# SSD sample block: stored-state and new-state products moved from the whole array to 32-wide strips

## The chip, the cores and the metric

The kernel runs on one core of a Trainium2 chip. The metric is the device time of one launch in microseconds (us). The kernel before took 1897.55 us, the median of three runs that went from 1896.7 to 1902.05 us.

## The reference

One step of a one-layer trunk is computed for 1024 new prompt rows and for 8 running streams of 16 rows each (128 sample rows, one block of 128). Three mixers run on the same normalised input: a stick-breaking attention, a Mamba-2 SSD group and a forgetting attention (FoX). Then come an output projection, a cross-attention into memory tokens, a SwiGLU feed-forward part and a last norm. Everything is float32.

The change touches the SSD mixer, and of it only the sample block. For a stream b and a head h with 64 channels p, a state of 128 numbers n, and the 16 rows t of the stream, the reference computes

```python
h0 = past['ssm']                                             # (8 streams, 8 heads, 64, 128)
y_off = einsum('bcthn,bchpn->bcthp', C, h_in) * exp(a_cum)   # what the stored state gives
chunk_states = einsum('bcshn,bcsh,bcshp->bchpn', B, to_end, x)
h_final = chunk_decay * h0 + chunk_states                    # the new state, an output
```

B and C are shared by the four heads of a group; there are two groups. So each stream has two products with its stored state (one for each group: 16 rows of C by 4 heads x 64 channels, contracted over the 128 state numbers) and, for the new state, a contraction over its 16 rows.

## The kernel before

The kernel is written with a tile framework: the program gives instructions in an order, and a planner, which runs a timeline of its own with costs for every instruction, sets the final order on each engine's queue. Instructions written earlier have the higher priority. `together` (L332) raises a list of matmuls far ahead in priority and has all but the first issued on the engine behind the first, so that they come out side by side. Buffers come from pools with a fixed number of slots; a tile takes a slot that is free and gives it back after its last reader. The PSUM pools matter here: `pd` has two banks (PD = 2), `pT` has three (PT_ = 3), `pS` two and `pO` one (L40). All DMAs are issued from one queue, SP's.

The attention of the prompt and of the streams (`pipeline`, L631) gives one step after another; between these steps L1296 to L1300 draw steps from a filler: first the remaining dense projections, then `ssd_gen` (L968). `ssd_gen` takes the sample block (i = 8) first and then the prompt blocks 0 to 7. For each block: `load` brings the conv output, the cumulated decays (as a broadcast from the scratch `ac_sc`, L1040) and the gate; `prepare` transposes; `weights` builds the decay weights (L1071 to L1087); `states` is the part with the stored state; `outputs` and `write` end it. The SBUF pool of `act` tiles has six slots; the two `st8` tiles with the stored states of four streams each are two of them, and a later block's load can take their slots only when the new states have been stored from them (L1145).

In `states`, for the sample block (L1104 to L1148), `cps[g]` is a zeroed 128 x 1024 area in which the 16 columns of C of stream b stand in a window of 128 columns for that stream, at the stream's own place among the 128 rows of the block. For each half hf of four streams:

- `bms` (L1121, POOL): B with the rows of all other streams zeroed, four streams side by side, 128 x 512, for each of the two groups. The area is used again in the second half.
- for each stream four transposes into a `pT` bank (L1129), an ACT copy to SBUF (L1131), and two products (L1133) that accumulate in the `pd` bank `yo` over all eight streams: a stationary 128 x 128 (mostly zeros) against 256 moving columns, each writing all 128 rows.
- for each of four head pairs j one product (L1140), 128 rows contracted, 128 x 128 stationary, 512 moving columns (four streams), into a `pd` bank, and four DVE instructions (L1143) that scale the old state and add the new part in place.
- one store of the half's 1 MB of new states (L1145).

A plain float32 matmul leaves two records in the trace, each with its weight load; a transpose leaves one. In the attention, `prompt_av` (L595) already issues products on two column strips of 64 and the stream attention (L874, L934) and the cross-attention (L1562) on four column strips of 32, all through `together`.

Of the kernel before, what the change touches and what calls it, by code (L numbers as in the profile page):

```python
# [12 lines left out]
ALU = mybir.AluOpType  # L13
# [4 lines left out]
P = 128  # L18
# [4 lines left out]
DEC_S = 16  # L23
# [39 lines left out]
def tile_hybrid_step(ctx: ExitStack, tc: tile.TileContext, a: dict):  # L63
    nc = tc.nc
    ACT, DVE, POOL, PE, SP = nc.scalar, nc.vector, nc.gpsimd, nc.tensor, nc.sync
# [20 lines left out]
    def act_t(dt=F32R, home=None):  # L86
        return (home or actp).tile([P, 3072], dt, tag="act", name="act")
# [13 lines left out]
    def sg_t(dt=F32):  # L101
        return sgp.tile([P, 512], dt, tag="sg", name="sg")
# [4 lines left out]
    def ps_t(pool, tag):  # L107
        return pool.tile([P, 512], F32, tag=tag, name="ps" + tag)

    def pd():  # L110
        return ps_t(psd, "d")
# [4 lines left out]
    def pT():  # L116
        return ps_t(pst, "t")
# [11 lines left out]
    def pool_tt(out, in0, in1, op):  # L129

        for a0, a1 in pieces_of(out.shape[1]):
            POOL.tensor_tensor(out=out[:, a0:a1], in0=in0[:, a0:a1], in1=in1[:, a0:a1], op=op)  # L132
# [19 lines left out]
    ident = cst.tile([P, P], F32, name="ident")  # L152
# [44 lines left out]
    maskh = mcst.tile([P, 2], F32, name="maskh")  # L197
# [134 lines left out]
    def together(emits):  # L332

        with tc.high_priority(GROUP):
            first = emits[0]()
            with tc.issue_after(first.ins):
                for f in emits[1:]:
                    f()
# [629 lines left out]
    def ssd_gen():  # L968
# [3 lines left out]
        bmask = sc[:, 1536:1544]  # L972
# [17 lines left out]
        for t_, pat in ((bo3, [0, DEC_S]), (bmask, None)):  # L990
            for sgn, base in ((-1, 0), (1, DEC_S - 1)):
# [6 lines left out]
                          in1=negA.unsqueeze(1).to_broadcast([P, NBLK, 8]), op=ALU.mult)  # L998
        POOL.tensor_copy(avx.rearrange("p (h d) -> p h d", d=64),
                         av[:, 64:72].unsqueeze(2).to_broadcast([P, 8, 64]))  # L1000
        ps = pd()
# [12 lines left out]
        ps = pd()  # L1014
# [7 lines left out]
        def h3(t):  # L1022
            return t.rearrange("p (h d) -> p h d", h=8)

        def bc(col, n=64):
            return col.unsqueeze(2).to_broadcast([P, 8, n])

        def heads_tt(out, x, col):

            for a0, a1 in pieces_of(512):  # L1030
                POOL.tensor_tensor(out=out[:, a0:a1].rearrange("p (h d) -> p h d", d=64),
                                   in0=x[:, a0:a1].rearrange("p (h d) -> p h d", d=64),
                                   in1=col[:, a0 // 64:a1 // 64].unsqueeze(2).to_broadcast([P, (a1 - a0) // 64, 64]),
                                   op=ALU.mult)

        def load(i):
            A = act_t(F32)
            SP.dma_start(out=A[:, 0:1024].rearrange("p (j t) -> p j t", t=P),
                         in_=xbc_sc[:, i * P:(i + 1) * P].rearrange("(j p) t -> p j t", p=P))
            SP.dma_start(out=A[:, 1024:2048],  # L1040
                         in_=ac_sc[8 * i:8 * i + 8, :].rearrange("h t -> (h t)").unsqueeze(0).to_broadcast([P, 1024]))
            SP.dma_start(out=A[:, 2048:2560], in_=z_sc[i * P:(i + 1) * P, :])
            return A

        def views(A, B):
            xT = A[:, 0:1024].rearrange("p (j t) -> p j t", t=P)
            return (xT, A[:, 1024:2048], A[:, 2048:2560], B[:, 0:256], B[:, 256:512],
                    *(B[:, 512 + 512 * k:1024 + 512 * k] for k in range(4)))
# [40 lines left out]
        def states(i, A, B, t1):  # L1089
            xT, br, zt, Bn, cb, xn, xd, xe, xD = views(A, B)  # L1090
            hs = slice(8 * i, 8 * i + 8)
            if i < 8:
                ps = pd()
                for g in range(2):
                    PE.matmul(ps[:, g * 256:(g + 1) * 256], xT[:, 6 + g, :], hT[:, g * 256:(g + 1) * 256],
                              start=True, stop=True)
                DVE.tensor_tensor(out=h3(t1), in0=h3(ps), in1=bc(ea[:, hs]), op=ALU.mult)
                heads_tt(hT, hT, dec[:, hs])
                ps = pd()
                for g in range(2):  # L1100
                    PE.matmul(ps[:, g * 256:(g + 1) * 256], Bn[:, g * P:(g + 1) * P], xe[:, g * 256:(g + 1) * 256],
                              start=True, stop=True)
                DVE.tensor_tensor(out=hT, in0=hT, in1=ps, op=ALU.add)
            else:  # L1104
                hs_, cps = [], []
                for g, t in enumerate(st8):
                    hst = t[:, :2048].rearrange("p (u n) -> p u n", n=P)

                    cp = t[:, 2048:3072]
                    POOL.memset(cp, 0.0)  # L1110
                    cv = bass.AP(cp.tensor, cp.offset, [list(cp.ap[0]), [144, 8], [1, 16]])
                    POOL.tensor_copy(cv, xT[:, 6 + g, :].rearrange("p (b t) -> p b t", t=DEC_S))
                    hs_.append(hst.rearrange("p (b j) n -> p b j n", j=4))
                    cps.append(cp)
                yo = pd()
                for hf in range(2):
                    hst = hs_[hf]
                    bms = []
                    for g in range(2):
                        bm = (A, B)[g][:, 2560:3072]  # L1120
                        POOL.tensor_tensor(out=bm.rearrange("p (b n) -> p b n", n=P),  # L1121
                                           in0=Bn[:, g * P:(g + 1) * P].unsqueeze(1).to_broadcast([P, 4, P]),
                                           in1=bmask[:, 4 * hf:4 * hf + 4].unsqueeze(2).to_broadcast([P, 4, P]), op=ALU.mult)
                        bms.append(bm)
                    for b in range(4):
                        bb = 4 * hf + b
                        tp = pT()
                        for j in range(4):
                            PE.transpose(tp[:, j * P:(j + 1) * P], hst[:, b, j, :], ident)  # L1129
                        h0 = sg_t()  # L1130
                        ACT.copy(h0, tp)  # L1131
                        for g in range(2):
                            PE.matmul(yo[:, g * 256:(g + 1) * 256], cps[g][:, bb * P:(bb + 1) * P],  # L1133
                                      h0[:, g * 256:(g + 1) * 256], start=bb == 0 and g == 0, stop=bb == 7,
                                      skip_group_check=True)
                        if b % 2 == 1:
                            yield
                    for j in range(4):
                        ps = pd()
                        PE.matmul(ps, xe[:, j * P:(j + 1) * P], bms[j // 2], start=True, stop=True)  # L1140
                        for b in range(4):
                            bb = 4 * hf + b
                            DVE.scalar_tensor_tensor(hst[:, b, j, :], hst[:, b, j, :], dcol[:, 8 * j + bb:8 * j + bb + 1],  # L1143
                                                     ps[:, b * P:(b + 1) * P], ALU.mult, ALU.add)
                    SP.dma_start(out=a["s_ssm"][0, 4 * hf:4 * hf + 4].rearrange("b h p n -> (b h p) n")  # L1145
                                 .rearrange("(u p) n -> p u n", p=P), in_=hst.rearrange("p b j n -> p (b j) n"))
                    yield
                DVE.tensor_tensor(out=h3(t1), in0=h3(yo), in1=bc(ea[:, hs]), op=ALU.mult)  # L1148
            pool_tt(t1, t1, xD, ALU.add)
# [23 lines left out]
        A, nxt = load(order[0]), None  # L1173
        B = act_t(F32)
# [8 lines left out]
        for n, i in enumerate(order):  # L1183
# [3 lines left out]
            if i == 7:  # L1187
                ps = pd()
# [18 lines left out]
            if n < 8:  # L1207
# [3 lines left out]
                A, B = A1, B1  # L1211
# [517 lines left out]
    B = {}  # L1729
# [335 lines left out]
```

## Time and profile before

| | |
|---|---|
| runs without a profile | 1897.55 us (1896.7 to 1902.05) |
| the profiled execution | 1900.41 us, of which the span of the profile is 1897.6 us |
| TensorE busy, as the profile counts it | 1832.7 us of the span |
| DVE, ACT, POOL busy | 890.6, 822.0, 618.0 us |
| stored-state products L1133 | 32 records, from 543.9 to 563.8 us |
| new-state products L1140 | 16 records, from 548.7 to 570.9 us |

PE is TensorE, PEld its weight loads, DVE VectorE, ACT ScalarE, POOL GpSimd and SPq the queue from which the DMAs are issued. A busy PE is not a PE at its peak, because the ends of pipelined matmuls are modelled: what a group of matmuls costs is read from the start of its first record to the start of the next instruction, not from its own duration. Windows are given in us from the start of the span.

### The profile page before, as it was taken

How to read it: one execution, taken by the hardware profiler on the slowest of the kernel's cores; microseconds unless marked ns; L12 is line 12 of the kernel's file. 1: busy time of each engine (PE TensorE's matmuls, PEld its weight loads, DVE VectorE, ACT ScalarE, POOL GpSimd, SP SyncE). 2: the span in 40 equal slices, each digit the busy share in tenths (PEclk: the TensorE clock that was granted, in tenths of full speed). 3: DMA queues.
4: the chain of work that ended last, by engine and by line, in shares of the span. 5: the costliest groups of instructions: out<-in, count | busy, mean ns of one | idle time of the engine just before them, and what ended most of it. 6: DMA issues, size and time to landing. Idle time of an engine off the chain costs nothing.

```text
span 1897.6 us, 32376 instructions
## 1 busy us (share of the span) xinstructions
PE 1832.7 (97%) x12120; PEld 1637.1 (86%) x12120; DVE 890.6 (47%) x1802; ACT 822.0 (43%) x1751; POOL 618.0 (33%) x923
## 2 busy tenths in 40 slices
PE   7999989999988899999999989999999999999998
PEld 5899878888966767899988879999999999788886
DVE  3412332566556863444444586333333333355554
ACT  6533543545567662344332474333333333344443
POOL 7622434535116652111112107445444542000000
PEclk9999999999999999999999999999999999999999
DMA  9464753537768773345576124333222233656572
GB/s 339 143 189 148 219 153 111 167 94 211 223 199 277 242 254 114 111 134 173 173 278 210 64 76 110 81 87 77 70 70 70 70 79 100 210 181 236 180 241 89
DMA packets 291069, 296.64 MB, mean 156 GB/s; under 512 B 80092, under 2 KB 242884, under 8 KB 290912
## 3 DMA queue, kind: packets, MB, share of 16 engines
q1 hardware_dynamic: 290912, 294.57, 49.6%
q8 instruction: 95, 1.56, 0.3%
q14 instruction: 62, 0.51, 0.1%
HBM read 225.12 MB, written 69.91 MB: 155 GB/s over the span
## 4 chain that ended last, share of the span: by engine, by line
PE 81%; DMA 7%; DVE 4%; POOL 4%; issue 2%; ACT 2%; SPq 1%; POOLq 0%; DVEq 0%; ACTq 0%
PE psd L1867 11%; PE psd L328 9%; PE psd L329 9%; PE psd L330 9%; PE pst L1867 8%; PE pss L1867 4%; PE pss L328 3%; PE pss L329 3%; PE pss L330 3%; POOL wl L132 2%; PE pso L1867 2%; PE pst L328 2%; PE pst L329 1%; PE pso L595 1%; PE pst L330 1%
## 5 line engine op out<-in xcount | busy, mean ns | idle before, releaser
L132 POOL TENSOR_TENSOR wl<-wr,wh 128x256 fp32r<-128x256 f32 (+2 forms) x184 | 138.8, 788 | 232.7 <-ACT wh L292 228.1
L330 PE MATMUL psd<-act,wl 128*128 128x384 f32 x528 | 180.8, 343 | 0.7 <-POOL wl L132 0.7
L328 PE MATMUL psd<-act,wh 128*128 128x384 f32 x528 | 181.4, 344 | 0.0
L329 PE MATMUL psd<-act,wh 128*128 128x384 f32 x528 | 180.7, 342 | 0.0
L1867 PE MATMUL pst<-bT,tr 128*128 128x256 f32 (+1 forms) x1068 | 155.0, 293 | 0.0
L1867 PEld LDWEIGHTS pst<-bT,tr 128*128 128x128 f32 x1068 | 144.9, 188 | 0.1
L330 PE MATMUL psd<-wh,act 128*128 128x512 f32 (+3 forms) x424 | 136.1, 322 | 0.0
L329 PE MATMUL psd<-wl,act 128*128 128x256 f32 (+3 forms) x414 | 133.5, 323 | 1.1 <-POOL wl L132 1.1
L328 PE MATMUL psd<-wh,act 128*128 128x256 f32 (+3 forms) x414 | 132.7, 324 | 1.2 <-DMA act<-osc 1.1
L1867 PE MATMUL psd<-bT,tr 128*128 128x320 f32 (+1 forms) x912 | 132.8, 295 | 0.6 <-POOL tr L132 0.6
L1867 PEld LDWEIGHTS psd<-bT,tr 128*128 128x128 f32 x912 | 124.8, 188 | 1.0 <-POOL tr L132 0.9
L132 POOL TENSOR_TENSOR tr<-u,tr 128x256 fp32r<-128x256 f32 x110 | 82.5, 779 | 101.2 <-ACT tr L1703 83.3
L253 POOL TENSOR_SCALAR sm<-sm 128x1 f32<-128x1 f32 (+2 forms) x27 | 7.1, 261 | 299.9 <-ACT y L1969 211.7
L1842 DVE TENSOR_TENSOR tr<-tr,pst 128x256 f32<-128x256 f32 (+1 forms) x86 | 38.6, 449 | 139.7 <-ACT tr L1839 106.4
L330 PEld LDWEIGHTS psd<-act,wl 128*128 128x128 f32 x528 | 99.2, 188 | 3.4 <-issue 1.9
L132 POOL TENSOR_TENSOR ws<-ws 128x256 f32<-128x256 f32 (+2 forms) x100 | 69.8, 725 | 98.3 <-DVE ws L522 85.2
L328 PEld LDWEIGHTS psd<-act,wh 128*128 128x128 f32 x528 | 99.4, 188 | 2.1 <-issue 1.6
L329 PEld LDWEIGHTS psd<-act,wh 128*128 128x128 f32 x528 | 99.3, 188 | 1.9 <-issue 1.5
L132 POOL TENSOR_TENSOR tr<-raw,tr 128x256 fp32r<-128x256 f32 x94 | 69.2, 766 | 83.6 <-ACT tr L1703 75.3
L1703 ACT CAST tr<-tr 128x384 fp32r<-128x384 f32 (+1 forms) x70 | 37.7, 538 | 117.3 <-DMA tr<-hidsc 114.0
L292 ACT CAST wh<-wr 128x512 fp32r<-128x512 f32 (+2 forms) x90 | 52.3, 621 | 81.3 <-PE psd L330 31.9
L328 PEld LDWEIGHTS psd<-wh,act 128*128 128x128 f32 x414 | 78.8, 191 | 9.9 <-issue 2.0
(637 smaller groups left out, 4763.5 us busy)
## 6 DMA issues: line engine op xcount, KB each, us to landing
u<-w_down SPq DMA_DIRECT2D x40, 512.0 KB
raw<-w_down SPq DMA_DIRECT2D x26, 512.0 KB
st<-qksc SPq DMA_DIRECT2D x48, 256.0 KB
wr<-w_in SPq DMA_DIRECT2D x44, 256.0 KB
tr<-hidsc SPq DMA_DIRECT2D x57, 192.0 KB
hidsc<-tr SPq DMA_DIRECT2D x34, 288.0 KB
qksc<-sg SPq DMA_DIRECT2D x48, 192.0 KB
wr<-cache_sb_k SPq DMA_DIRECT2D x32, 256.0 KB
```

The source lines that it names most:

```text
L132: POOL.tensor_tensor(out=out[:, a0:a1], in0=in0[:, a0:a1], in1=in1[:, a0:a1], op=op)
L253: POOL.tensor_scalar(v, ss, inv, EPS, ALU.mult, ALU.add)
L292: ACT.copy(hi, raw)
L328: PE.matmul(out, ah, bh, start=start, stop=False)
L329: PE.matmul(out, ah, bl, start=False, stop=False)
L330: PE.matmul(out, al, bh, start=False, stop=stop)
L595: return PE.matmul(po[r:r + 64, q_], vt[:, 2 * (k0 + i) + j, :], pfs[i][:, sl], start=start and k0 == 0 and (j == 0 or qp > 0), stop=k0 + ...
L1703: ACT.copy(hi, src)
L1842: DVE.tensor_tensor(out=at(out, g), in0=at(x, g), in1=ps[g][:, :GW[g]], op=op)
L1867: PE.matmul(dst[g][:, :GW[g]], x[:, ka], y[:, k, :], start=start and k == 0 and m == 0, stop=stop and k == 3 and m == 2, skip_group_check= ...
```

## The change

The new `states` for the sample block, of which only this part differs:

```diff
-                    cp = t[:, 2048:3072]
+                    cp = t[:, 2048:2304]
                     POOL.memset(cp, 0.0)
-                    cv = bass.AP(cp.tensor, cp.offset, [list(cp.ap[0]), [144, 8], [1, 16]])
-                    POOL.tensor_copy(cv, xT[:, 6 + g, :].rearrange("p (b t) -> p b t", t=DEC_S))
+                    cv = bass.AP(cp.tensor, cp.offset, [list(cp.ap[0]), [64, 4], [48, 2], [1, 16]])
+                    POOL.tensor_copy(cv, xT[:, 6 + g, :].rearrange("p (i e t) -> p i e t", e=2, t=DEC_S))
...
+                bms = []
+                for g in range(2):
+                    bm = (A, B)[g][:, 2560:2816]
+                    POOL.tensor_tensor(out=bm.rearrange("p (e n) -> p e n", n=P),
+                                       in0=Bn[:, g * P:(g + 1) * P].unsqueeze(1).to_broadcast([P, 2, P]),
+                                       in1=maskh.unsqueeze(2).to_broadcast([P, 2, P]), op=ALU.mult)
+                    bms.append(bm)
                 for hf in range(2):
                     hst = hs_[hf]
-                    bms = []
-                    for g in range(2):
-                        bm = (A, B)[g][:, 2560:3072]
-                        POOL.tensor_tensor(out=bm.rearrange("p (b n) -> p b n", n=P),
-                                           in0=Bn[:, g * P:(g + 1) * P].unsqueeze(1).to_broadcast([P, 4, P]),
-                                           in1=bmask[:, 4 * hf:4 * hf + 4].unsqueeze(2).to_broadcast([P, 4, P]), op=ALU.mult)
-                        bms.append(bm)
-                    for b in range(4):
-                        bb = 4 * hf + b
-                        tp = pT()
-                        for j in range(4):
-                            PE.transpose(tp[:, j * P:(j + 1) * P], hst[:, b, j, :], ident)
-                        h0 = sg_t()
-                        ACT.copy(h0, tp)
-                        for g in range(2):
-                            PE.matmul(yo[:, g * 256:(g + 1) * 256], cps[g][:, bb * P:(bb + 1) * P],
-                                      h0[:, g * 256:(g + 1) * 256], start=bb == 0 and g == 0, stop=bb == 7,
-                                      skip_group_check=True)
-                        if b % 2 == 1:
-                            yield
+                    for e in range(2):
+                        h0 = []
+                        for b in (e, 2 + e):
+                            tp = pT()
+                            for j in range(4):
+                                PE.transpose(tp[:, j * P:(j + 1) * P], hst[:, b, j, :], ident)
+                            h0.append(sg_t())
+                            ACT.copy(h0[-1], tp)
+                        together([lambda r=32 * (2 * hf + x), g=g, x=x: PE.matmul(
+                            yo[r:r + 32, g * 256:(g + 1) * 256], cps[g][:, 2 * r + 32 * e:2 * r + 32 * e + 32],
+                            h0[x][:, g * 256:(g + 1) * 256], start=e == 0 and g == 0, stop=e == 1, skip_group_check=True)
+                            for g in range(2) for x in (1, 0)])
+                        yield
                     for j in range(4):
-                        ps = pd()
-                        PE.matmul(ps, xe[:, j * P:(j + 1) * P], bms[j // 2], start=True, stop=True)
+                        pss_ = [pd(), pT()]
+                        together([lambda r=32 * (2 * hf + x), x=x: PE.matmul(
+                            pss_[x][:, :256], xe[r:r + 32, j * P:(j + 1) * P], bms[j // 2][r:r + 32, :],
+                            start=True, stop=True) for x in range(2)])
```

Two neighbouring streams share a strip of 32 rows. For the products with the stored state, C of a stream stands in a window of 32 columns (the other stream's 16 are zero), and the result goes to the 32 rows of the strip alone. The two streams that are taken together lie in different strips: streams 0 and 2, then 1 and 3, and likewise in the second half. For the new state, only the 32 rows of the strip are contracted, against B with one of the two streams zeroed in each half of 256 columns (`maskh` in place of `bmask`); the two strips of a half write to two banks, one from `pd` and one from `pT`. The DVE instructions keep their number and shape and read from the two banks in turn. B is masked once for all streams and both halves. The number of transposes, copies, steps of the filler and DMAs stays as it was; there are eight more `pT` tiles, sixteen new-state matmuls in place of eight, and the products are issued through `together`.

More of the change, by code (lines that the diff above doesn't have):

```diff
@@ L1143, in states @@
                             DVE.scalar_tensor_tensor(hst[:, b, j, :], hst[:, b, j, :], dcol[:, 8 * j + bb:8 * j + bb + 1],
-                                                     ps[:, b * P:(b + 1) * P], ALU.mult, ALU.add)
+                                                     pss_[b // 2][:, b % 2 * P:(b % 2 + 1) * P], ALU.mult, ALU.add)
                     SP.dma_start(out=a["s_ssm"][0, 4 * hf:4 * hf + 4].rearrange("b h p n -> (b h p) n")
```

## The prediction

> **What bounds the kernel now.** I read the page first, then the busy time by stretches of ten microseconds around the sample block, then the order of PE's instructions there, then what PE and the DMA queue wait for.
>
> ```profile
> PE 1832.7 (97%) x12120; PEld 1637.1 (86%) x12120; DVE 890.6 (47%) x1802; ACT 822.0 (43%) x1751; POOL 618.0 (33%) x923
> ...
> PE 81%; DMA 7%; DVE 4%; POOL 4%; issue 2%; ACT 2%; SPq 1%; POOLq 0%; DVEq 0%; ACTq 0%
> ```
>
> Over the whole span PE sets the time: work taken from PE is worth its length wherever nothing else ends later. The chain is 19% other things, though, and the sample block lies in a stage where these matter:
>
> ```profile
> core 0: us, PE busy (x) PEld busy (x) DVE busy (x) ACT busy (x) POOL busy (x), PEclk, DMA share, GB/s
> 500.00:740.00 240.00, 219.06 (x1659) 171.38 (x1658) 146.16 (x405) 145.47 (x313) 111.49 (x183) 0.96 0.74 235
> ...
> 530.00:540.00 10.00, 6.19 (x47) 4.94 (x45) 5.83 (x25) 7.45 (x21) 5.46 (x8) 0.94 0.64 194
> 540.00:550.00 10.00, 9.71 (x41) 7.28 (x42) 5.60 (x20) 5.02 (x11) 0.00 (x0) 0.72 0.24 61
> 550.00:560.00 10.00, 9.24 (x112) 7.11 (x111) 7.25 (x25) 4.03 (x9) 1.04 (x1) 1.00 0.59 169
> 560.00:570.00 10.00, 10.00 (x52) 6.30 (x51) 6.79 (x24) 9.79 (x21) 2.46 (x3) 1.00 1.04 274
> 570.00:580.00 10.00, 8.10 (x63) 6.72 (x62) 3.69 (x12) 5.01 (x10) 4.05 (x7) 1.00 0.97 314
> ```
>
> From 500 to 740 us PE is idle for 240 - 219 = 21 us, a third of all its idle time (1897.6 - 1832.7 = 65). Before 540 it stands still, then has a low clock; from 560 on the DMA engines are full (1.04, 0.97). PE's order there, with the idle time ahead of an instruction in brackets:
>
> ```profile
> 540.29 0.58 PE L562 MATMUL pss<-st 128*128 128x256 f32 x1 [4.09 <-DVE sm L536]
> ...
> 543.94 2.73 PE L1133 MATMUL psd<-sg,act 128*128 128x256 f32 x8
> 546.32 0.58 PE L562 MATMUL pss<-st 128*128 128x512 f32 x1
> ...
> 552.79 1.12 PE L1140 MATMUL psd<-act 128*128 128x512 f32 x2
> ...
> 556.77 1.10 PE L1140 MATMUL psd<-act 128*128 128x512 f32 x2 [0.76 <-DVE so L959]
> ...
> 572.76 1.31 PE L889 MATMUL pst<-ident,wr 128*128 128x128 f32 x8 [1.32 <-DMA wr<-cache_fox_k]
> ```
>
> So the block's products lie between three stops of PE: 4.09 us before 540.29, 0.76 before 556.77 and 1.32 before 572.76.
>
> **The change part by part.** First what the products cost now. The time of a group runs from its start to that of the next instruction:
>
> ```profile
> 558.14 1.03 PE L1133 MATMUL psd<-sg,act 128*128 128x256 f32 x4
> 559.00 0.60 PE L1129 MATMUL pst<-ident,act 128*128 128x128 f32 x4
> 559.44 0.49 PE L580 MATMUL pst<-ident,ws 128*128 128x128 f32 x3
> ...
> 560.63 1.02 PE L1140 MATMUL psd<-act 128*128 128x512 f32 x2
> 561.49 0.59 PE L1133 MATMUL psd<-sg,act 128*128 128x256 f32 x2
> ```
>
> Four records of L1133 take 559.00 - 558.14 = 0.86 us, 0.215 each; two of L1140 take 561.49 - 560.63 = 0.86, 0.43 each. Thus 32 records of the first cost 6.9 us and 16 of the second 6.9. The first eight of L1133 ran at the low clock: 546.32 - 543.94 = 2.38 instead of 1.72.
>
> *Stored-state products.* After the change they are still 32 records of 256 moving columns, in four groups of eight, each on two column strips in turn. Two column strips in turn are in the trace, in the prompt's attention:
>
> ```profile
> 525.89 1.08 PE L595 MATMUL pso<-pt,st 128*64 128x256 f32 x8
> 526.90 0.88 PE L580 MATMUL pst<-ident,ws 128*128 128x128 f32 x6
> 527.71 0.65 PE L595 MATMUL pso<-pt,st 128*64 128x256 f32 x4
> 528.28 0.65 PE L580 MATMUL pst<-ident,ws 128*128 128x128 f32 x4
> ...
> 895.56 1.07 PE L1562 MATMUL pss<-kf,ws 128*32 128x256 f32 x16
> 896.56 0.39 PE L328 MATMUL pss<-kt,st 128*128 128x256 f32 x1
> ```
>
> Eight records take 526.90 - 525.89 = 1.01, four take 0.57. Half of the serial time would be 0.86 and 0.43; so each group pays 0.14 to 0.15 on top. Strips of 32 do it too: L1562 has sixteen records on four strips in 1.00. Price: 4 x 1.01 = 4.0; saved 3 x (1.72 - 1.01) = 2.1, and for the group at the low clock 2.38 x (1 - 1.01/1.72) = 1.0, together **3.1 us**. Bounds: a loss of 0.6 (four times 0.15) if nothing overlaps, a gain of 3.4 + 0.3 (half of 6.9, and half of the low clock's 0.66) if all does.
>
> The Trainium skill, TensorEngine Tiling (Array Packing), section Key Properties, has a rule against this: changing the tiling mode drains the array. The 0.14 us on each group of L595 is what this trace shows beside it, and it is in the price already, twelve times for the twelve new groups; without it the saving would be 1.7 us larger.
>
> *New-state products.* After the change there are 32 records (16 matmuls) of 256 moving columns in eight groups of four, on two row strips of 32 with 128 stationary columns. No row has two row strips side by side. The nearest by shape is a single matmul with 32 rows, in a stretch with clock 0.50:
>
> ```profile
> 283.11 0.79 PE L726 MATMUL psd<-so,hsel 32*128 32x128 f32 x2
> 283.83 0.80 PE L562 MATMUL pss<-st 128*128 128x512 f32 x1
> ```
>
> Its two records take 0.72 us at half speed, 0.36 at full, where two of 0.11 (L1129's transposes: 0.44 for four) and a group's 0.14 make the same: a row strip is no slower in itself. Ends: no overlap, 32 x 0.215 + 8 x 0.14 = 8.0, a loss of 1.1; full overlap 3.4, a gain of 3.4. I take the column strips' four-record group, 0.57, as nearest in shape of group: 8 x 0.57 = 4.6, saved **2.3 us**.
>
> *What lies beside other work.* POOL's masks and memsets:
>
> ```profile
> L1121 POOL TENSOR_TENSOR act<-act x4: 1038/1039/1039, 537.0 to 561.8; 128x512 f32<-128x512 f32 x4
> ...
>   PE psd L1140: 15.0, 1
> ...
> L1110 POOL MEMSET act<- x2: 950/1196/1442, 511.2 to 520.6; 128x1024 f32 x2
> ```
>
> Four masks of 1.04 become two of half the size, and the memsets shrink to a quarter: about 2 x 1.2 x 3/4 + 4.2 - 1.1 = 4.9 us less on an engine that is busy 2.46 of 10 us here. The 15.0 us that the second half's mask waited for the last product on the old one disappears; but its last mask ended at 562.8, and the second half's first product started at 565.37 (quoted below), so nobody waited for it: zero. Without that cover one mask, 1.04, would be at stake. DVE's 32 instructions (L1143, 0.28 us from start to start), the transposes, copies and DMAs stay: zero.
>
> *What of the 5.4 us is kept.* Up to the stop at 556.77 the cut is two stored-state groups (1.0 + 0.7) and two new-state groups (0.6): 2.3 us. There the DMA share is 0.24 and 0.59, and what the stop waits for (L959 on DVE) comes from PE's own stream attention, which moves up with the rest: I keep all. Behind it the cut is 1.4 + 6 x 0.29 = 3.1 us, and it runs into a stop on a load:
>
> ```profile
> 565.37 1.02 PE L1140 MATMUL psd<-act 128*128 128x512 f32 x2
> ...
> 565.56 7.06 DMA wr<-cache_fox_k
> ...
> 574.28 7.19 DMA s_ssm<-act
> 581.53 0.38 SPq L1038
> 581.96 6.43 DMA act<-acsc
> ```
>
> With full DMA engines the 7.06 us of that load do not start earlier just because PE asks earlier; PE would wait longer than 1.32. What can move is the second store of the states: the chain runs over it and the load into its slot to 588.4. I keep a quarter, 0.8. Sum: 2.3 + 0.8 = **3.1 us**. The profiled execution took 1900.41 us (2.8 outside its span), so 1897.3 in its like; the median of the runs is 2.9 lower than that execution, so **1894.5**.
>
> **The rivals.** *(a) The stop at 540 goes with it.* The planner lays this stage out anew. PE's 4.09 us wait for FoX's DVE work (L536), which stands on DVE behind L1080, which waits for `ac_sc`:
>
> ```profile
> L1080 DVE TENSOR_SCALAR act<-act x45: 268/279/1002, 538.1 to 667.6; 128x128 f32<-128x128 f32 x45
> ...
>   DMA act<-acsc: 6.8, 4
> ```
>
> The clock then was 0.72 over ten microseconds, 2.8 us more, together 6.9. Is another layout free of it, the time is 1897.55 - 3.1 - 6.9 = **1887.5**. For it: products in high priority change PE's order from here on. Against it: nothing in the diff touches that load or L1080. The Trainium skill, TensorE: Matmul & The Clock Gate, Part 1, has the array's clock fall to half after an idle window of about 3.4 us; here 4.09 us of idle are followed by the low clock and 1.32 us are not, which agrees.
>
> *(b) All of it is kept.* If the stage is PE's after all: 1897.55 - 5.4 = **1892.1**. For it speaks 10.00 of 10 busy in 560 to 570, against it the DMA share.
>
> *(c) Nothing is kept*, because pairs are not side by side (the planner gives a pair's second bank only when one is free) or because the saved time becomes waiting for `cache_fox_k`: **1897.5**.
>
> *(d) The third bank is missing.* A new-state pair now holds a `pT` bank until DVE has read it. In the first half successive pairs are 556.77 - 552.79 = 4.0 us apart; so for 16 us one of three banks is out of the attention's hands, and with two pairs open in the second half, two of three. A tile of transposes needs 0.44 us on PE and then a copy:
>
> ```profile
> L1131 ACT COPY sg<-pst x8: 562/573/592, 531.6 to 561.1; 128x512 f32<-128x512 f32 x8
> ```
>
> With one bank a tile comes every 0.44 + 0.57 = 1.0 us, 0.6 more than now. About ten tiles lie in the second half (seven of `cache_fox_k`, 28 records of L889, and some of L580): 6 us; and if one wait of over 4 us comes of it, 2.8 by the clock. Net -3.1 + 9 = +6: **1903.5**, slower. It decides from the point where DVE leaves a bank unread for over 3 us. For it: DVE does FoX's rows between (7.25 of 10 busy). Against it: the planner knows the banks and can put other work ahead.
>
> **How the numbers follow.** Chances: forecast 0.28, (a) 0.18, (b) 0.15, (c) 0.17, (d) 0.22. A measurement of this kernel tells about 0.3% (5.7 us) from no change: below 1891.9 is faster, above 1903.2 slower. Faster: all of (a), half of (b), and 0.06 from the forecast's low side, 0.32. Slower: two thirds of (d) and 0.06 of rearrangements that no row prices, 0.21. The same: 0.47. The range reaches from just below (a), 1886, to (d), 1904; the likeliest case's own range is 1891 to 1897.
>
> **What would show it.** In the changed profile: L1133 as 128*32 with eight records in about 1.0 us from start to start; L1140's line as 32*128 with four in 0.43 to 0.86; L1121 two times, about 0.55 us each. The gain is where I put it if the second store of the states is issued 2 to 5 us earlier against 540.29 and PE's stop on `cache_fox_k` grows. (d) shows as transposes (L580, L889) waiting for DVE's L1143 line, (a) as no stop above 3 us with a clock of 1.00 through 540 to 550. I am wrong if groups come out one by one, if row strips cost 0.43 a record, or if stops elsewhere, up to the end of this stage at 740 us, change by more than the block itself.

## The result and the profile after

The changed kernel takes 1888.83 us (median of six runs, 1882.73 to 1892.76) against 1901.41 us for the kernel before (six runs, 1896.7 to 1905.48, the three from ahead of the prediction among them): ratio 0.9926, 95% interval 0.9906 to 0.9946. A ratio here is the one on record, which is not quite the quotient of the two medians (it differs from it by up to 1.5 us). It was timed twice more, with 0.9954 (0.9937 to 0.9972) and 0.9935 (0.9914 to 0.9955). So it is faster by 9 to 14 us; the forecast was 3.

In the diff's new text the lines behind the block move down by two: the DVE instructions are L1145, the store L1147, the outputs L1157, the output of the feed-forward L1869; the masks are L1119 and the transposes L1130. The page of the changed kernel (its own time 1882.73 us):

```profile
span 1881.0 us, 32406 instructions
...
PE 1821.7 (97%) x12136; PEld 1628.8 (87%) x12136; DVE 892.0 (47%) x1802; ACT 822.5 (44%) x1751; POOL 613.0 (33%) x921
```

PE is busy for 11.0 us less than the 1832.7 before, and the span is 16.6 us shorter. This execution is the fastest of its six runs, 6.1 us under their median. The stretches around the block, columns as in the prediction:

```profile
500.00:740.00 240.00, 222.62 (x1729) 173.30 (x1728) 152.21 (x412) 148.86 (x319) 107.09 (x183) 1.00 0.74 237
530.00:540.00 10.00, 9.68 (x73) 7.18 (x72) 7.54 (x32) 9.40 (x24) 4.66 (x8) 1.00 0.61 168
540.00:550.00 10.00, 9.94 (x112) 6.74 (x111) 8.97 (x30) 6.20 (x13) 0.00 (x0) 1.00 0.36 100
```

The two stretches with idle time and a low clock before, 530 to 550, now have 9.68 and 9.94 of 10 us busy and a clock of 1.00 (before: 6.19, 9.71, with 0.94 and 0.72). From 500 to 740 the clock is 1.00 throughout and PE is idle for 17.4 us, before 20.9. PE's instructions in order of time (start, duration, what; the idle time ahead in brackets):

```profile
538.34 1.06 PE L1133 MATMUL psd<-sg,act 128*32 128x256 f32 x8 [0.32 <-POOL act L1119]
539.33 0.74 PE L925 MATMUL pst<-ident,ws 128*128 128x128 f32 x4
...
540.76 0.69 PE L1140 MATMUL psd<-act 32*128 32x256 f32 x2
541.38 0.44 PE L563 MATMUL pss<-st 128*128 128x384 f32 x1
...
549.07 0.48 PE L1140 MATMUL pst<-act 32*128 32x256 f32 x1
549.09 0.48 PE L1140 MATMUL psd<-act 32*128 32x256 f32 x1
...
549.61 1.61 PE L1140 MATMUL pst<-act 32*128 32x256 f32 x6
551.15 1.54 PE L1130 MATMUL pst<-ident,act 128*128 128x128 f32 x12
...
558.01 0.67 PE L1140 MATMUL psd<-act 32*128 32x256 f32 x2 [0.78 <-DVE act L1145]
558.61 1.06 PE L1133 MATMUL psd<-sg,act 128*32 128x256 f32 x8
559.60 0.48 PE L1140 MATMUL pst<-act 32*128 32x256 f32 x1
```

No stop of 4 us is left in this stretch. The column strips are there (538.34: eight records on 128*32, 0.99 us to the next start). Of the row strips (32*128) some stand alone (540.76: two records, 0.62 us), some side by side (549.07 and 549.09, the first of four records that start by twos: 0.54 us to 549.61).

Where the time went is best read from the attention's last stage as a whole, from the start of the block's first matmul (L1002) to the first instruction of the next stage on DVE (L1389, now L1391). One row for each execution, columns as above; first before, then after, then the same changed kernel in its two other sessions:

```profile
520.50:713.10 192.60, 172.87 (x1375) 132.23 (x1374) 129.98 (x373) 131.26 (x285) 98.72 (x157) 0.96 0.76 245
```

```profile
522.00:700.80 178.80, 162.79 (x1379) 122.71 (x1378) 129.78 (x369) 130.31 (x284) 94.02 (x155) 1.00 0.80 262
```

```profile
527.10:711.50 184.40, 167.66 (x1378) 125.82 (x1377) 130.69 (x369) 130.72 (x284) 94.47 (x155) 0.97 0.77 253
```

```profile
524.00:706.50 182.50, 165.39 (x1379) 125.60 (x1378) 131.12 (x369) 130.93 (x284) 93.96 (x155) 0.98 0.79 257
```

I split each length in three: PE's idle time (length less busy), the time that a low clock costs (length times one less the granted clock, known to about 1 us because the clock has two digits), and the rest, which is PE's work at full clock. The time after the stage is the span less the row's end.

| execution | span | stage starts | stage | idle | low clock | work | after the stage |
|---|---|---|---|---|---|---|---|
| before | 1897.6 | 520.5 | 192.6 | 19.7 | 7.7 | 165.2 | 1184.5 |
| after | 1881.0 | 522.0 | 178.8 | 16.0 | 0 | 162.8 | 1180.2 |
| after, second session | 1892.9 | 527.1 | 184.4 | 16.7 | 5.5 | 162.1 | 1181.4 |
| after, third session | 1887.1 | 524.0 | 182.5 | 17.1 | 3.7 | 161.7 | 1180.6 |

The gain has four parts: some 3 us of work (2.4, 3.1, 3.5), some 3 us of idle time (3.7, 3.0, 2.6), 2 to 8 us of low clock, and 3 to 4 us behind the stage. The first is what the products save (about 2.5 us by their rows at full clock: 13.8 before, 3.9 and 7.3 after). The other three are waits and their consequences, and the third differs by 5.5 us between executions of the same program; of the kernel before there is one trace only. The start of the stage differs too (from 520.5 to 528.0 over all profiles, 522.0 to 527.1 for the changed kernel), so that the spans of single executions don't measure the gain; the medians do.

The order of two other queues has changed with it. On DVE (before, then after):

```profile
538.12 1.79 DVE L1080 TENSOR_SCALAR act<-act 128x128 f32<-128x128 f32 x5 [3.28 <-DMA act<-acsc]
...
539.90 0.33 DVE L536 CUSTOM_DVE_ANT_0 ws<-pss,ws,sm 128x128 f32<-128x128 f32 x1
```

```profile
535.05 0.35 DVE L536 CUSTOM_DVE_ANT_0 ws<-pss,ws,sm 128x128 f32<-128x128 f32 x1
...
537.50 0.36 DVE L1080 TENSOR_SCALAR act<-act 128x128 f32<-128x128 f32 x1 [1.34 <-DMA act<-acsc]
```

Before, five L1080 stood ahead of the last piece of L536 and waited for the load of `ac_sc`; PE waited for that piece. Now L536 is done at 535.4 and L1080 waits alone. On SP's queue (before, then after):

```profile
564.81 0.54 SPq L1145 DMA_DIRECT2D s_ssm<-act  x1
565.56 4.38 SPq L883 DMA_DIRECT2D wr<-cache_fox_k  x2
...
570.60 0.54 SPq L883 DMA_DIRECT2D wr<-cache_fox_k  x1
...
571.79 1.95 SPq L883 DMA_DIRECT2D wr<-cache_fox_k  x2
...
574.28 0.43 SPq L1145 DMA_DIRECT2D s_ssm<-act  x1
...
581.53 0.38 SPq L1038 DMA_DIRECT2D act<-xbcsc  x1
```

```profile
552.93 0.38 SPq L1147 DMA_DIRECT2D s_ssm<-act  x1
...
563.85 0.38 SPq L1147 DMA_DIRECT2D s_ssm<-act  x1
564.53 4.54 SPq L883 DMA_DIRECT2D wr<-cache_fox_k  x3
...
569.73 0.53 SPq L1038 DMA_DIRECT2D act<-xbcsc  x1
```

Before, five loads of `cache_fox_k` were issued between the block's two stores; the second store came at 574.28 and the load of a prompt block behind it (L1038) at 581.53. Now no such load stands between the stores; the second is issued at 563.85, that block load at 569.73, 11.8 us earlier in the span. Three waits of PE over the whole span (total us, times, longest), before and after:

```profile
PE pst L889 <- DMA wr<-cache_fox_k: 5.2, 4, 2.5
PE pst L1867 <- ACT u L1752: 2.9, 1, 2.9
...
PE psd L328 <- ACT tr L1703: 2.2, 1, 2.2
```

```profile
PE pst L1869 <- ACT u L1754: 2.1, 1, 2.1
...
PE pst L889 <- DMA wr<-cache_fox_k: 1.4, 1, 1.4
...
PE psd L328 <- ACT tr L1705: 0.9, 1, 0.9
```

The waits for `cache_fox_k` fall from 5.2 to 1.4 us. The one right behind the block hardly changes (1.32 us before, 1.4 now); the longest, 2.51 us at 623.78, is gone. The other two lie at the feed-forward, far behind the change; they fall from 5.1 to 3.0 us and are part of what is gained behind the stage.

### The profile page after: what moved, and what is told of

Same layout as the page of the kernel before. It is cut to its first block, busy times and chain, and to the rows that moved or that the text cites. A ratio compares the mean times of both kernels' runs of the same rounds, so it can differ in the third digit from the quotient of the medians.

```text
span 1881.0 us, 32406 instructions
## 1 busy us (share of the span) xinstructions
PE 1821.7 (97%) x12136; PEld 1628.8 (87%) x12136; DVE 892.0 (47%) x1802; ACT 822.5 (44%) x1751; POOL 613.0 (33%) x921
## 4 chain that ended last, share of the span: by engine, by line
PE 62%; DMA 3%; DVE 2%; ACT 2%; issue 1%; POOL 1%; SPq 0%; DVEq 0%; POOLq 0%; ACTq 0%
PE psd L1869 11%; PE pst L1869 8%; PE psd L328 5%; PE psd L329 5%; PE psd L330 5%; PE pss L1869 4%; PE pss L328 3%; PE pss L329 3%; PE pss L330 3%; PE pso L1869 2%; PE pst L328 1%; PE pst L329 1%; PE pst L330 1%; PE pso L328 1%; PE pso L330 1%
## 5 line engine op out<-in xcount | busy, mean ns | idle before, releaser
L1869 PE MATMUL pst<-bT,tr 128*128 128x256 f32 (+1 forms) x1068 | 155.0, 293 | 0.0
L1869 PEld LDWEIGHTS pst<-bT,tr 128*128 128x128 f32 x1068 | 144.9, 188 | 0.1
L1869 PE MATMUL psd<-bT,tr 128*128 128x320 f32 (+1 forms) x912 | 133.0, 295 | 0.4 <-POOL tr L132 0.4
L1869 PEld LDWEIGHTS psd<-bT,tr 128*128 128x128 f32 x912 | 125.1, 189 | 0.7 <-POOL tr L132 0.7
L329 PEld LDWEIGHTS psd<-wl,act 128*128 128x128 f32 x414 | 79.2, 191 | 9.3 <-POOL wl L132 4.1
```

Of the source, the lines that this page charges most:

```text
L329: PE.matmul(out, ah, bl, start=False, stop=False)
L1869: PE.matmul(dst[g][:, :GW[g]], x[:, ka], y[:, k, :], start=start and k == 0 and m == 0, stop=stop and k == 3 and m == 2, skip_group_check= ...
```

## The experiments

Three explanations were tried against each other: the strips themselves (work on PE), the stop at 540 that went away (an order on DVE, which would follow from the smaller memset on POOL), and the order that the planner gives to everything behind the block. A ratio below is against the kernel before on the same chip in the same session, with its 95% interval; gains in us are one minus the ratio, times the median of the kernel before there (1904.16, 1903.13 and 1904.22 us in the experiments' three sessions).

### The small memset alone

The kernel before, with its memset cut in two; the columns beyond 256 are cleared by DVE.

```diff
-                    POOL.memset(cp, 0.0)
+                    POOL.memset(cp[:, :256], 0.0)
+                    DVE.memset(cp[:, 256:], 0.0)
```

> The kernel before, with all its products on the whole array; only the memset of the two areas for C is cut in two: 256 columns stay on POOL, as many as the changed kernel clears there, and the other 768 go to DVE. The planner then puts FoX's last row piece (L536) ahead of the decay weights (L1080) on DVE, as in the changed kernel. Theory ORDER (the gain is the 4.1 us stop of PE at 540 us, the low clock behind it and what follows from it, and comes of the planner's shorter POOL cost): 7 to 12 us faster than before, the stop gone, clock 1.00 from 540 to 550. Theory ARRAY (the gain is the strips' shorter time on PE): no change, within 3 us.

Measured 1902.05 us, ratio 0.9983 (0.9969 to 0.9996): 3.2 us faster. Lines from 1111 on are one further down. DVE's order:

```profile
537.35 0.35 DVE L536 CUSTOM_DVE_ANT_0 ws<-pss,ws,sm 128x128 f32<-128x128 f32 x1
...
539.96 0.71 DVE L1080 TENSOR_SCALAR act<-act 128x128 f32<-128x128 f32 x1 [1.98 <-DMA act<-acsc]
```

L536's piece now ends ahead of L1080, as in the changed kernel, though no product was touched: PE's stop of over 4 us is gone. So a memset on POOL, for which the trace shows nobody waiting, decides by its length the order on DVE; the next run shows it from the other side. In all profiles it goes with the memset: the four kernels with the long one on POOL have the stop (4.1 to 5.3 us), the others do not. The stop alone is worth about 3 us of the kernel's time (0.8 to 5.9), less than the 6.9 us that it and its low clock took in one execution, and less than the 7 to 12 of theory ORDER.

### The changed kernel with the long memset

```diff
-                    POOL.memset(cp, 0.0)
+                    POOL.memset(t[:, 2048:3072], 0.0)
```

> The changed kernel, with both strips, but its memset clears 1024 columns as before (768 of them are used by nobody). The planner then puts L1080 ahead of L536 again. ORDER: the stop of about 4 us and the clock of 0.7 from 540 to 550 are back, and of the 12 to 14 us of gain only what the array saves is left, 2 to 5 us against before. ARRAY: 10 to 14 us faster than before, as the changed kernel.

Measured 1895.64 us, ratio 0.9953 (0.9935 to 0.9970): 8.9 us faster than before. DVE's order and PE's stop:

```profile
544.02 1.07 DVE L1080 TENSOR_SCALAR act<-act 128x128 f32<-128x128 f32 x5 [4.31 <-DMA act<-acsc]
...
545.08 0.33 DVE L536 CUSTOM_DVE_ANT_0 ws<-pss,ws,sm 128x128 f32<-128x128 f32 x1
```

```profile
545.47 0.58 PE L562 MATMUL pss<-st 128*128 128x256 f32 x1 [4.41 <-DVE sm L536]
```

The old order and the stop are back, 4.41 us long, and still most of the gain stays. The stop is a part of it, between 0 and 5 us by the changed kernel's three measurements (8.8, 12.4 and 14.1 us), but not the cause of the whole. The gain lies between what the two theories expected, 2 to 5 and 10 to 14 us.

### One kind of strip at a time

Column strips with the small memset, and new states as before; then the other way round: row strips, masks made once and the second bank from `pT`, with stored states and memset as before. Each is the part of the change's diff that its name says.

```diff
 # column strips only (L1109 to L1137 of the changed kernel; the new states stay)
+                        together([lambda r=32 * (2 * hf + x), g=g, x=x: PE.matmul(
+                            yo[r:r + 32, g * 256:(g + 1) * 256], cps[g][:, 2 * r + 32 * e:2 * r + 32 * e + 32],
...
 # row strips only (masks, L1138 to L1146; the stored states stay)
+                        together([lambda r=32 * (2 * hf + x), x=x: PE.matmul(
+                            pss_[x][:, :256], xe[r:r + 32, j * P:(j + 1) * P], bms[j // 2][r:r + 32, :],
...
```

> Column strips for the stored states alone, with their smaller memset; the new states as before, on the whole array with two masks a half and one bank. ORDER: no stop at 540, 9 to 14 us faster than before, nearly all of the gain or more, since the row strips' groups took about 7.3 us in the changed kernel's trace against 6.9 before. ARRAY: about half of the gain, 6 us.

> Row strips for the new states alone, masks once for both halves, a pd and a pT bank each; the stored states as before with the large memset. ORDER: the stop at 540 stays, within 3 us of before. ARRAY: about half of the gain, 6 us faster.

Column strips: 1901.46 us, 0.9981 (0.9967 to 0.9995), 3.6 us faster, about what the memset gives alone. Row strips: 1902.24 us, 0.9988 (0.9975 to 1.0002), no difference that can be told. The sum of the two, 6 us, is less than the change gives together; ORDER's 9 to 14 us for the column strips did not come, and ARRAY's 6 us for each half is above both values, for the column strips just inside the interval (1.0 to 6.3). What PE waits for in the row-strip kernel, 515 to 590 us:

```profile
PE pss L562 <- DVE sm L536: 5.3, 1, 5.3
PE psd L1140 <- DVE act L1145: 2.9, 2, 2.0
```

Here the stop of 5.3 us is there, and PE also waits 2.9 us for the DVE instructions that free the new states' banks: the wait of the prediction's rival (d), in a kernel without the other half of the change. The column-strip kernel's stage:

```profile
526.30:715.60 189.30, 170.57 (x1361) 127.24 (x1361) 130.33 (x373) 130.15 (x283) 98.82 (x157) 0.96 0.77 247
```

Up to the next block's first product (L1095, at 574.9) it is 48.6 us long, 10.9 less than before (520.5 to 580.0). Over the whole stage there are 18.7 us idle, 7.6 at the low clock and 163.0 of work, and it is only 3.3 us shorter: what the block gives, the rest of the stage takes back here. The same split of the stage in every profile supports the saved work: the eight kernels and repeats with column strips have 160.4 to 163.0 us of work, 161.8 in the mean, the six without 161.9 to 165.9, in the mean 164.5.

### The changed kernel again

> The changed kernel once more, beside the next three on the same chip. 10 to 16 us faster than before; clock near 0.992 against 0.988. In its trace the block, from the first product of the decays (L1002) to the first state product of prompt block 0 (L1095), takes about 47 us, against 59.5 before, 53.3 with the memset alone cut, 53.5 with both strips and the large memset, 48.7 with the column strips and the small memset. The rest of the stage, on to the second half of the output projection (L1391), took 131 us here and 132 to 140 in the others.

> The changed kernel beside the other three: 8 to 14 us faster than before, clock 0.989 to 0.992, time multiplied by the clock near 1872 us against 1880 before.

The first: 1893.94 us, 0.9954 (0.9937 to 0.9972). The second: 1892.60 us, 0.9935 (0.9914 to 0.9955). With the first measurement that is a gain in each of three sessions; its size is known to no better than some 3 us, and the 10 to 16 us expected of the first of the two were not reached. The block took 49.8 and 47.9 us, 47.0 in the first profile, and the rest of the stage 134.6 in both, against 131.8 there and 133.1 before.

### The order without strips, and strips without the order

First the kernel before with the split memset, its whole-array products issued through `together` in the changed kernel's order of streams (0 and 2, then 1 and 3). Then the changed kernel with `together` replaced by a plain loop.

```diff
 # order without strips
+                        together([lambda g=g, x=x, bb=4 * hf + 2 * x + e: PE.matmul(
+                            yo[:, g * 256:(g + 1) * 256], cps[g][:, bb * P:(bb + 1) * P],
...
+                        together([lambda: PE.matmul(ps, xe[:, j * P:(j + 1) * P], bms[j // 2], start=True, stop=True)])
 # strips without the order (the same for the new states)
+    def apart(emits):
+        for f in emits:
+            f()
-                        together([lambda r=32 * (2 * hf + x), g=g, x=x: PE.matmul(
+                        apart([lambda r=32 * (2 * hf + x), g=g, x=x: PE.matmul(
...
```

> The kernel before with the memset cut in two as in the first run, and all its products on the whole array issued in the changed kernel's order, through together. Theory BLOCK (the block gets shorter by about 6 us through the stop and by about 6 through the strips, and the rest of the stage keeps or loses it as the planner lays it out): block near 53 us, 2 to 7 us faster than before. Theory GROUP (the high priority of the products makes the gain): 10 to 14 us faster.

> The changed kernel with its strips but without together: the products have no raised priority and are not bound to each other. BLOCK: pairs come out side by side only in part, the block takes 48 to 52 us; 5 to 13 us faster than before, depending on the rest of the stage. GROUP: all or most of the gain is gone, 0 to 4 us.

The order without strips is slower: 1907.53 us, 1.0023 (1.0006 to 1.0040). Strips without `together`: 1894.29 us, 0.9953 (0.9935 to 0.9971), the same as the changed kernel in that session (0.9954). The high priority is not what gains. The first run came out against both theories, and its block took 58.2 us instead of 53. In the second the block took 48.7 us, as BLOCK expected, and its trace has the same three groups of row strips side by side as the changed kernel's: `together` is not what puts them there.

### The second bank instead of row strips

Column strips and small memset as in the change; the new states stay on the whole array with the old masks, but each product is cut in two of 256 columns, one into a `pd` bank and one into a `pT` bank. It was run in two sessions.

```diff
-                        ps = pd()
-                        PE.matmul(ps, xe[:, j * P:(j + 1) * P], bms[j // 2], start=True, stop=True)
+                        pss_ = [pd(), pT()]
+                        together([lambda x=x: PE.matmul(
+                            pss_[x][:, :256], xe[:, j * P:(j + 1) * P], bms[j // 2][:, 256 * x:256 * x + 256],
+                            start=True, stop=True) for x in range(2)])
```

> Column strips and small memset; the new states on the whole array with the masks of before, but with 256 columns in a pd bank and 256 in a pT bank for each head pair, through together, as the changed kernel does with its row strips. If the row strips themselves are what lifts 3.6 us (column strips alone) to 14: 2 to 6 us faster than before. If it is the second bank and the priority: 9 to 14 us. The block takes 48 to 50 us either way, and 32 records of 256 columns cost 32 x 0.215 = 6.9 us.

> Column strips, small memset, new states on the whole array in two banks, once more beside the changed kernel. If the row strips are worth nothing: 8 to 12 us faster than before and no slower than the changed kernel, 0 to 3 us faster. If they are worth the forecast's 2.3 us, the changed kernel is ahead by that.

Measured 1890.50 us, 0.9940 (0.9923 to 0.9958), and 1892.87 us, 0.9933 (0.9913 to 0.9953): as fast as the changed kernel beside it (0.9954 and 0.9935). There is no row strip in it. Its new-state products (records, busy us, mean ns):

```profile
L1140 PE MATMUL psd<-act 128*128 128x256 f32 x16 | 5.0, 394 | 0.1
L1140 PE MATMUL pst<-act 128*128 128x256 f32 x16 | 4.5, 396 | 0.0
```

So the row strips give nothing that two banks on the whole array don't give. From the column-strip kernel this one differs in the second bank and in what goes with it (the product cut in two, issued through `together`); it gains 8 us more (11.4 against 3.6, in two sessions). Its stage:

```profile
524.90:706.30 181.40, 164.15 (x1377) 125.46 (x1376) 130.25 (x369) 130.85 (x284) 96.98 (x157) 0.99 0.80 259
```

Idle 17.2, low clock 1.8, work 162.3: 1.5, 5.8 and 0.7 us less than with column strips alone. On SP's queue two `cache_fox_k` loads stand between the block's stores in the column-strip kernel, none in this one.

### The second bank alone, without any strip

The same edit of the new states in the kernel before; first with its memset as it was, then with the split memset.

> The kernel before, stored states and new states on the whole array, large memset; only the new states of a head pair are written as two products of 256 columns, one to a pd and one to a pT bank, through together. Theory LAYOUT (the second bank lets the planner lay out the rest of the stage in another way, worth 5 to 6 us of time at full clock, and the strips are worth little): 4 to 8 us faster than before, the stop at 540 still there, block 58 to 60 us. Theory BLOCK (the gain is stop plus strips, 6 us each): no change, within 3 us.

> The same with the memset cut in two as in the first run: no strip at all, but the stop gone and the second bank. LAYOUT: 8 to 12 us faster than before, as much as the changed kernel. BLOCK: 3 to 6 us, from the stop alone; block near 53 us.

Measured 1897.90 us, 0.9964 (0.9948 to 0.9980), 6.9 us faster, and 1899.59 us, 0.9973 (0.9961 to 0.9985), 5.1 us faster. Neither theory stands whole. By the layout theory the second, without strips, should have been worth 8 to 12 us; it was worth 5, and that is what the block theory gave it (3 to 6). By the block theory the first, whose stop is still there (4.28 us before PE's L562), should have been worth nothing; it was worth 7, inside the layout theory's 4 to 8. The parts don't add: the second bank gives 7 us alone, 2 beside the split memset (5.1 against 3.2), 8 beside the column strips; the column strips give nothing beside the memset (3.6 against 3.2) and 6 to 8 us beside both (11.4 and 12.8 against 5.1). By the intervals the 7 and the 2 can't be told apart (3.8 to 9.9 for the second bank alone, 2.9 to 7.4 for it with the split memset); the two larger steps, with column strips and second bank together, are clear. In the profiles the blocks of the column strips alone and of the second bank with the split memset are short too, 48.6 and 50.7 us, but the rest of their stage takes 140.7 and 141.5 us against 133.1 before.

In all kernels with the second bank no `cache_fox_k` load is issued between the block's stores; in those without it there are five (before, split memset, order without strips) or two (column strips). That order goes with the gain, but isn't enough for it: the row-strip kernel has it too, and its 2.3 us (0.4 slower to 4.8 faster) can't be told from nothing. No run isolated it. No kernel beat the changed one clearly.

## Why the prediction was right or wrong

**Direction and range** were right: faster, and 1888.83 lies in 1886 to 1904. The size was wrong: 3.1 us forecast, 9 to 14 measured, and the likeliest case did not come about. That the time lies in the range is in part luck. It lies near rival (a)'s 1887.5, whose stop did go, but the stop accounts for about 3 us and not for 6.9; the rest goes with an order of the queues for which the sum has no term and which no run isolated.

**Column strips** came out as costed. Four groups of eight records took 0.98 to 0.99 us each (two of them at 538.34 and 558.61 above) against 1.01. The price was taken from the attention's column strips, the right row.

**Row strips** are the term of the sum that failed first: 2.3 us saved was forecast, about 0.4 us is lost. From start to start the 32 records took 7.3 us (0.62, 0.60, 0.59, 0.62, 0.54, 1.54, 0.54, 0.60, 0.53, 0.52, 0.62; the second 0.54, ahead of an idle time, is taken from the first) against 6.9 before. It is what rival (c) names, pairs that are not side by side: the `pT` half mostly comes later than the `pd` half. That its bank comes free late is (c)'s reason for it; no run shows the reason. At 540.76 a `pd` half runs alone; at 549.61 three `pT` halves follow one another. Three groups of four are really side by side and take 0.54 us, near the 0.57 of the column strips. The others pay a group's surcharge each without its gain: a matmul alone takes about 0.60, which is 0.43 and 0.17 more. The prices were near, then (the prediction took 0.14 from L595's groups and found it again in L726's row), and the sum lies within the bound for no overlap, 8.0; what was wrong is that all eight pairs were taken as pairs. The Trainium skill, TensorEngine Tiling (Array Packing), Key Properties, says that changing the tiling mode drains the array: the 0.17 us on each matmul that stands alone agrees with it. It need not be the whole of it: the three that follow one another from 549.61 on take 0.51 each, still 0.08 more than 0.43.

**What lies beside other work** was costed at zero for POOL, and as POOL's time that was right: POOL is busy for 5.0 us less (618.0 to 613.0), and nothing waited for it before. What was missed is that the length of these instructions enters the planner's timeline and so the order on DVE. Rival (a) was argued against with "nothing in the diff touches that load or L1080"; the split memset alone shows that the memset was enough. The trace shows both signs of (a): no stop above 3 us, clock 1.00 from 540 to 550. Its price was too high, though: 6.9 us in the one execution, 3.2 us by the runs of the split memset, and putting the stop back into the changed kernel left 8.9 us of gain.

**What is kept** was the next failing step. The prediction kept a quarter of what is cut behind the stop at 556.77, because loads of `cache_fox_k` on full DMA engines would not come earlier, and PE's wait for them would grow. That took SP's order as fixed. In the changed kernel the second store stands ahead of these loads, 10.4 us earlier in the span; counted from the matmul that stood behind the stop (540.29, now 535.89) it is 6.0 us, where 2 to 5 was forecast. PE's wait for the loads fell from 5.2 to 1.4 us over the span and stayed as it was right behind the block. In the first profile the stage gives nothing back: up to the next block's first product (L1095, 580.04 before, 568.98 after) the stage is 12.5 us shorter, over its whole length 13.8 us. In the two other profiles of the changed kernel it gives back 1.5 us, 9.7 and 11.6 becoming 8.2 and 10.1. With the column strips alone the prediction's picture holds: there the stage gives most of it back.

**Rival (d)** didn't come about: PE waits 0.78 us in all for a bank that DVE has to free (558.01). In the row-strip kernel it was 2.9 us, so the wait exists, below the price of 6 us.

What stays open is why the column strips give nothing beside the small memset alone and 6 to 8 us once the second bank is there too. The order of the queues behind the block differs in each, and single executions differ by several us in their low clock; which of the changed places carries the difference no run has shown.

## What to carry to other kernels

Where a planner sets the order, an edit can be worth more through the order that it triggers than through its own work: leave the products as they are, make the small side edits (a memset's length, a second PSUM bank) alone first, and compare queue orders before costing the main edit. Look in the trace whether pairs written for two row strips come out side by side: here three groups of four records did and the others paid the surcharge alone, and a second bank on the whole array gave the same time. Measure a change of this size in several sessions, since one profile of a kernel differs from the next by some 10 us of span.

## What the runs showed that was not expected

**The same stop costs a half clock in one execution and not in another.** In the changed kernel PE waits 2.70 us for DVE at the same instruction in each of its three profiles. The first profile, PE's row and the stretches of two us around it:

```profile
668.28 1.06 PE L874 MATMUL pss<-kf,act 128*32 128x512 f32 x8 [2.70 <-DVE sm L536]
...
669.99 1.90 PE L1157 MATMUL psd<-act 128*128 128x64 f32 x16
```

```profile
668.00:670.00 2.00, 1.72 (x15) 0.92 (x16) 2.00 (x5) 0.25 (x1) 2.00 (x4) 1.00 1.05 401
670.00:672.00 2.00, 2.00 (x21) 2.00 (x20) 1.88 (x8) 1.50 (x3) 1.38 (x3) 1.00 1.02 304
```

The second session's, the same program:

```profile
675.72 1.07 PE L874 MATMUL pss<-kf,act 128*32 128x512 f32 x8 [2.70 <-DVE sm L536]
...
677.88 3.52 PE L1157 MATMUL psd<-act 128*128 128x64 f32 x16
```

```profile
676.00:678.00 2.00, 2.00 (x16) 1.29 (x8) 2.00 (x6) 0.37 (x1) 2.00 (x4) 0.74 0.99 386
678.00:680.00 2.00, 2.00 (x12) 2.00 (x11) 1.30 (x4) 1.77 (x3) 0.82 (x2) 0.50 0.96 353
```

In the first the clock stays at 1.00; in the second it falls to 0.74 and then 0.50 from just behind the stop, and L1157's sixteen records take 3.52 us there against 1.90 in the first. By the table above such falls cost 0, 5.5 and 3.7 us of the stage in three executions of one program, and 7.7 in the kernel before. In the third session a stop of 2.19 us (557.43) is followed by no fall and one of 1.88 us (579.26) by a clock of 0.50. The Trainium skill, TensorE: Matmul & The Clock Gate, section What's actually happening, says that the clock follows an activity window that runs freely, which fits: what a stop costs would then depend on where in the window it falls. Its figure for an idle window is about 3.4 us; here shorter stops, of 2.70 and 1.88 us, were enough once each, so the stop's own length does not decide it. For the prediction this means that a stop of 2 to 3 us has an expected price above its length, which the rule used there (4.09 us is followed by the low clock, 1.32 us not) left out. The trace of the kernel before already had such a stop between the two, with a clock of 0.53 in the two us from 624 on:

```profile
623.78 0.77 PE L889 MATMUL pst<-ident,wr 128*128 128x128 f32 x4 [2.51 <-DMA wr<-cache_fox_k]
```
